# Attention of a two-layer trunk: B projected as 384 columns twice, q and k normalised at another place and by VectorE alone, two chunks of transposed probabilities in one PSUM bank

## The chip, the cores and the metric

One core of one Trainium2 chip runs the whole program in one launch. The metric is the device time of an execution in microseconds (us). The program uses five engines: TensorE (PE in the profile, with its weight loads as PEld), VectorE (DVE), ScalarE (ACT), GpSimd (POOL), and SyncE (SP), which here only issues DMAs.

## The reference, cut to what matters

The input is 512 tokens of width 1024 in float32. Layer 0 has two kinds of attention on one normalised input: A, 8 heads of 64 with a mixture of three dilated windows, and B, 8 query heads over 2 key-value heads, a window of 128 and a learned sink per head. Layer 1 has 16 heads of forgetting attention, called C here. Each layer ends with an MLP of width 4096 with a squared ReLU.

```python
q = rms_norm(q.reshape(bsz, seq, heads, 64), q_gain)   # A, B and C; k in the same way
s = q @ k * 64**-0.5 + bias                            # window, slope, or forget gates
p = exp(s - max(s));  out = (p @ v) / sum(p)           # B: the sink joins max and sum
y = concat(a_out, b_out) @ w_out                       # layer 0; layer 1: c_out @ w_out
x = x + y;  x = x + square(relu(rms_norm(x) @ w_up)) @ w_down
```

So every head of q and k (not v) is divided by its own root mean square before the scores are taken.

## The kernel before, in words

**Number format.** Each float32 operand is split into a high part (`hi`, a cast to fp32r) and a low part (`lo`, the rest), and a product is three matmuls: high by high, low by high, high by low. So weights and activations pass through a cast on ScalarE or GpSimd and a subtraction on VectorE or GpSimd before TensorE can use them (`split` L146, `scale_split` L156).

**Order.** The kernel is traced in Python, and a planner then orders each engine's instructions: every instruction has a priority, by default the order in which it was traced, and the planner takes, engine by engine, the one of the best priority that it thinks is ready, by costs of its own. Instructions marked `keep_in_program_order` stay in traced order; in the attention hardly any are. At run time each engine is strictly in order and waits at the first instruction whose inputs are late. DMAs of weights and of K stand in SyncE's one queue.

**Projections.** `project` (L206) takes some columns of the input weights and gives four banks of PSUM (tag pA, 4 banks in all), one for each 128 tokens. It walks over the 1024 rows in groups of `kw` chunks of 128 (4 chunks for 256 columns, else 2); `load_w` (L177) issues one DMA per group and column range into a raw tile (4 raw tiles in all, `RAW`) and splits it into high and low. The engines of the splits come from a pattern: `PAT_START` casts on ScalarE and subtracts on VectorE, `PAT_ATT` casts on GpSimd and subtracts on VectorE or GpSimd in turn.

**Normalisation.** `norm_heads` (L239) takes the four banks when they are complete. For each it copies the bank to SBUF and squares it, both on ScalarE from PSUM, and sums the squares by head on VectorE (L249). Then come four small scalings (L252), an inverse root by bit trick and three Newton steps on VectorE (`rsqrt_small`, L122, 11 instructions), and four multiplications in place (L259), which `NORM = 'vgvg'` gives to VectorE and GpSimd in turn.

**Attention.** `attend` (L402) goes by pairs of heads. `prep_q` and `prep_k` transpose normalised columns on TensorE into a PSUM bank (tag pB, 4 banks), split them, and for k copy the halves to the other partitions by DMA (L289). `scores` (L301) handles four blocks of 128 queries: scores on TensorE, bias and row minimum of the negated scores on VectorE (L338), exponential with row sum on ScalarE (L341), a reciprocal of that block's sum on VectorE (L344), and a scaling of the probabilities, on GpSimd for blocks 0 to 2 and on ScalarE for block 3 (`PSC = 'ggga'`). `values` (L352) of the head before then transposes the probabilities by chunk of 128 keys: four chunks, four PSUM banks, each with its cast on ScalarE (L373) and subtraction on VectorE (L374); after that it multiplies with V (L381) and evicts (L384, L385). In A and C the chunks 0 to 3 are 512, 384, 256 and 128 columns wide, in B 256, 256, 256 and 128. Chunk 3 is multiplied together with 128 columns of zeros that lie before it in tile `p3`.

**Interleaving.** `run` (L429) traces one attention generator beside one generator of dense matmuls. A dense step counts 32 by its columns over 32 (a projection of n columns counts n in all), an attention step counts one, and `run` keeps `d / n_dense` level with `a / n_att` plus a lead. A step ends at each `yield`: one for each pair, four for the scores of a head, and one for each bank of `values` and its product. In layer 0 the order is: `qk_a(0)` (q and k of A's heads 0 to 3), `v_a(0)`; then attention A of those heads beside `kv_b` (256 columns) and B's q (512 columns); then attention B (`n_att` is `NB` = 86) beside `qk_a(1)` and `v_a(1)` (768 columns); then attention A of heads 4 to 7 beside the output projection. In layer 1 three such runs of C, each beside the projections of the next four heads, and one beside the output projection.

Of the kernel before, what the change touches and what calls it, by code (L numbers as in the profile page):

```python
# [14 lines left out]
OP = mybir.AluOpType  # L15
# [22 lines left out]
NORM = 'vgvg'  # L38
PSC = 'ggga'
GRAIN = 4  # L40
STARTPIN = 4
# [30 lines left out]
def trunk(ctx, tc, x, g_mix, g_mlp, w_in_even, a_q_gain, a_k_gain, b_q_gain, b_k_gain, b_sinks,  # L72
# [45 lines left out]
    ecol = consts.tile([P, NT], F32, name="ecol")  # L118

# [71 lines left out]
    def layer_attention(li, hT, w_in, w_out, stats=None):  # L191


        with ExitStack() as c2:
# [9 lines left out]
            nc.gpsimd.memset(p3[:, :, 256:384].bitcast(F32), 0.0)  # L204
# [34 lines left out]
            def norm_heads(outs, nh, sq_tag="sq", sq_bufs=1 + li):  # L239
# [61 lines left out]
            def scores(q, k, j, kind, h, pr):  # L301
# [11 lines left out]
                rden = small.tile([P, NT], F32, tag="rden", name="rden")  # L313
                for i in range(NT):
# [29 lines left out]
                    nc.vector.reciprocal(rden[:, i:i + 1], den[:, i:i + 1])  # L344
                    if PSC[i] == "a":
                        nc.scalar.activation(p[:, :nv], p[:, :nv], AF.Copy, scale=rden[:, i:i + 1])
                    else:
                        eng = nc.gpsimd if PSC[i] == "g" else nc.vector
                        eng.tensor_scalar(p[:, :nv], p[:, :nv], rden[:, i:i + 1], 1.0, op0=OP.mult, op1=OP.mult)  # L349
                    yield  # L350

            def values(pr, kind, V, vs, yf, j):  # L352

                pts = []
                for c in range(NT):
                    pt = bank("pB", "PT")
                    blocks = [i for i in range(c, NT) if kind != "b" or i <= c + 1]
                    n = len(blocks) * P
                    for i in blocks:
                        kb = c - (max(i - 1, 0) if kind == "b" else 0)  # L360
                        nc.tensor.transpose(pt[:, (i - c) * P:(i - c + 1) * P],  # L361
                                            pr[i][:, kb * P:(kb + 1) * P], ident)
                    if c < 2:
                        d = ap.tile([P, 2, 512 - c * P], F32R, tag=f"PT{c}", bufs=1, name="PT")
                        dst, rhs = d[:, :, :n], d[:, :, :n]
                        cols = slice(c * P, c * P + n)
# [878 lines left out]
```

## Time and profile before

| | |
|---|---|
| median of 3 runs | 1168.81 us (1167.73 to 1170.11) |
| the profiled execution | 1168.43 us |
| its span, first instruction to last | 1166.7 us |
| PE busy / DVE / ACT / POOL | 98% / 75% / 55% / 17% of the span |
| granted TensorE clock | 0.999 in the mean |

The span is the time from the first to the last instruction on the chip; 1.7 us of the execution's time lie around it. Busy shares are averages over stages that differ much. Attention with its projections lies at 28 to 230 us (layer 0) and at 600 to 820 us (layer 1); the MLPs and output projections fill most of the rest. Within layer 0, A's first four heads end at about 105 us, B's heads lie at about 105 to 175 us, and A's last four end at about 210 us. A wait in the view of waits is idle time of an engine before one instruction, with the releaser that came last. Matmuls are pipelined, and their recorded lengths overlap: what one costs TensorE is read from the distance of two starts.

### The profile page before, as it was taken

The numbers are of one execution on the slowest core, as the hardware profiler recorded it, in microseconds if no ns is written. First come the engines' busy times: TensorE is split into PE (matmuls) and PEld (weight loads), VectorE is DVE, ScalarE is ACT, GpSimd is POOL, SyncE is SP. The second block draws the span as 40 slices with busy tenths as digits, with TensorE's granted clock in tenths as the row PEclk, the third lists the DMA queues.
The fourth block names the chain that finished last, engine by engine and source line by source line (L and its number), as shares of the span: only waits on it lengthen the run. The fifth ranks groups of instructions, "written<-read, shape, count | busy, mean of one in ns | idle before, by whom it ended". The sixth has DMA issues, their size and how long they took to land.

```text
span 1166.7 us, 17503 instructions
## 1 busy us (share of the span) xinstructions
PE 1146.8 (98%) x6256; PEld 982.5 (84%) x6256; DVE 880.7 (75%) x1877; ACT 647.1 (55%) x1349; POOL 202.4 (17%) x296
## 2 busy tenths in 40 slices
PE   8999989999999999999999999999999999999998
PEld 7987877888988988988887888888888888888887
DVE  7878999968858857855647877788858759669676
ACT  6555867556545545444235675656756455465452
POOL 1345444200000000000255445332100000000000
PEclk9999999999999999999999999999999999999999
DMA  7522014242333333333443333343430721623403
GB/s 253 163 76 89 19 57 146 70 126 78 104 108 91 91 108 91 106 111 110 146 128 109 107 84 109 107 118 113 163 105 4 235 87 55 198 73 109 147 33 109
DMA packets 100655, 126.57 MB, mean 108 GB/s; under 512 B 6184, under 2 KB 79944, under 8 KB 100568
## 3 DMA queue, kind: packets, MB, share of 16 engines
q1 hardware_dynamic: 99384, 121.23, 34.3%
q10 hardware_dynamic: 608, 2.13, 0.5%
q0 software_dynamic: 576, 2.10, 0.4%
q8 instruction: 49, 0.80, 0.3%
q14 instruction: 38, 0.31, 0.1%
HBM read 112.29 MB, written 6.32 MB: 102 GB/s over the span
## 4 chain that ended last, share of the span: by engine, by line
PE 85%; DVE 8%; DMA 2%; POOL 1%; issue 1%; ACT 1%; SPq 0%; ACTq 0%; POOLq 0%; DVEq 0%
PE up L163 10%; PE up L167 10%; PE up L166 10%; PE pj L230 5%; PE pj L232 5%; PE pj L231 5%; PE O L381 3%; PE PT L361 2%; PE Y L1021 2%; PE Y L1019 2%; PE Y L1022 2%; PE op L167 2%; PE op L163 2%; PE op L166 2%; PE Y L1068 1%; PE S L324 1%
## 5 line engine op out<-in xcount | busy, mean ns | idle before, releaser
L163 PE MATMUL up<-xin,whi 128*128 128x512 f32 x512 | 200.5, 392 | 0.0
L167 PE MATMUL up<-xin,whi 128*128 128x512 f32 x512 | 199.3, 389 | 0.0
L166 PE MATMUL up<-xin,wlo 128*128 128x512 f32 x512 | 199.2, 389 | 0.0
L768 ACT CAST whi<-wraw 128x512 fp32r<-128x512 f32 x228 | 139.2, 619 | 105.0 <-PE up L167 47.7
L769 DVE TENSOR_TENSOR wlo<-wraw,whi 128x512 fp32r<-128x512 f32 x228 | 151.7, 686 | 50.8 <-ACT whi L768 50.5
L167 PEld LDWEIGHTS up<-xin,whi 128*128 128x128 f32 x512 | 96.1, 188 | 20.1
L166 PEld LDWEIGHTS up<-xin,wlo 128*128 128x128 f32 x512 | 96.2, 188 | 19.8 <-issue 0.2
L163 PEld LDWEIGHTS up<-xin,whi 128*128 128x128 f32 x512 | 96.1, 188 | 19.8 <-issue 0.2
L341 ACT ACTIVATE P<-P,negm 128x128 f32<-128x128 f32 (+5 forms) x128 | 69.5, 544 | 51.7 <-DVE negm L338 47.9
L950 ACT ACTIVATE u<-up 128x512 f32<-128x512 f32 x64 | 38.3, 599 | 90.9 <-PE up L167 90.8
L230 PE MATMUL pj<-whi,hn 128*128 128x512 f32 (+2 forms) x256 | 88.7, 346 | 0.0
L232 PE MATMUL pj<-whi,hn 128*128 128x512 f32 (+2 forms) x256 | 86.9, 339 | 0.0
L231 PE MATMUL pj<-wlo,hn 128*128 128x512 f32 (+2 forms) x256 | 86.8, 339 | 0.0
L151 POOL TENSOR_SCALAR whi<-wraw 128x512 fp32r<-128x512 f32 x88 | 60.5, 689 | 143.0 <-PE pj L232 121.8
L789 DVE TENSOR_TENSOR t<-u 128x256 f32<-128x256 f32 x56 | 23.2, 424 | 62.8 <-ACT u L1093 61.0
L154 POOL TENSOR_TENSOR wlo<-wraw,whi 128x512 fp32r<-128x512 f32 x48 | 64.4, 1346 | 20.7 <-ACT whi L149 17.9
L230 PE MATMUL pj<-whi,h 128*128 128x512 f32 (+1 forms) x192 | 66.5, 353 | 0.7 <-DVE v L159 0.7
L232 PE MATMUL pj<-whi,h 128*128 128x512 f32 (+1 forms) x192 | 65.5, 343 | 0.0
L231 PE MATMUL pj<-wlo,h 128*128 128x512 f32 (+1 forms) x192 | 65.5, 341 | 0.0
L349 POOL TENSOR_SCALAR P<-P,rden 128x256 f32<-128x256 f32 (+2 forms) x96 | 47.7, 500 | 90.8 <-DVE rden L344 90.0
L154 DVE TENSOR_TENSOR wlo<-wraw,whi 128x512 fp32r<-128x512 f32 (+1 forms) x72 | 49.9, 700 | 17.7 <-POOL whi L151 14.5
L373 ACT CAST PT<-PT 128x256 fp32r<-128x256 f32 (+3 forms) x128 | 49.5, 405 | 19.4 <-PE PT L361 18.5
(229 smaller groups left out, 3054.4 us busy)
## 6 DMA issues: line engine op xcount, KB each, us to landing
wraw<-in_w_up SPq DMA_DIRECT2D x64, 512.0 KB, 3.8
wraw<-in_w_down SPq DMA_DIRECT2D x56, 512.0 KB, 4.2
wraw<-in_w_in_odd SPq DMA_DIRECT2D x36, 256.0 KB, 3.3
mraw<-in_w_down SPq DMA_DIRECT2D x16, 512.0 KB, 4.4
K<-K SPq DMA_DIRECT2D x26, 256.0 KB
wraw<-in_w_in_even SPq DMA_DIRECT2D x10, 512.0 KB, 4.0
wraw<-in_w_in_even SPq DMA_DIRECT2D x16, 256.0 KB, 4.5
xl<-xsp SPq DMA_DIRECT2D x8, 512.0 KB
```

What stands on the lines that cost most here:

```text
L151: nc.gpsimd.tensor_scalar(dst_h, src, 1.0, 1.0, op0=OP.mult, op1=OP.mult)
L154: in_order((nc.gpsimd if lo == "pool" else nc.vector).tensor_sub(dst_l, src, dst_h.bitcast(F32)))
L163: m = nc.tensor.matmul(o, wh, xh, start=start, stop=False, skip_group_check=more)
L166: nc.tensor.matmul(o, wl, xh, start=False, stop=False, skip_group_check=more)
L167: nc.tensor.matmul(o, wh, xl, start=False, stop=stop, skip_group_check=more)
L230: nc.tensor.matmul(o, xh, hi[:, :n], start=k == 0, stop=False)
L231: nc.tensor.matmul(o, xh, lo[:, :n], start=False, stop=False)
L232: nc.tensor.matmul(o, xl, hi[:, :n], start=False, stop=k == DC - 1)
L341: nc.scalar.activation(p[:, :ne], p[:, :ne], AF.Exp, scale=-1.0, bias=negm[:, i:i + 1], accum_out=den[:, i:i + 1])
L373: nc.scalar.copy(dst[:, 0], pt[:, :n])
L768: sca(nc.scalar.copy(dst_h, src))
L769: late.append(lambda: vec(nc.vector.tensor_sub(dst_l, src, dst_h.bitcast(F32))))
```

## The change

Four edits, all in the attention of both layers.

1. `norm_heads` first copies the four banks (ScalarE). All the rest is traced at once, but under `later(100)`, which raises the priority number by 100: the planner ranks it behind the next 100 traced instructions or so. The squares are taken from the copy in SBUF. The four small scalings become one instruction over all four token blocks, and all four multiplications go to VectorE.
2. B's projection is cut differently. Before: k and v of B (256 columns), then q of B (512 columns). After: q heads 0 to 3 with k (384 columns, `PAT_START`), then q heads 4 to 7 with v (384 columns, `PAT_ATT`). A group of rows then has two DMAs, of 256 and 128 columns.
3. In `scores` the reciprocals and scalings of blocks 0 to 2 come together after block 2's exponential; block 3's follow after its own. A head has two reciprocals where it had four.
4. In `values` A and C put chunks 3 and 2 into one bank, so three banks, casts and subtractions where there were four. B puts chunks 0 and 1 into one and 3 and 2 into another: two where there were four. The zeros in `p3` move to its first 128 columns. A head of A or C has one step fewer, a head of B two fewer; `NB`, `LEADS` and the other counts of `run` stay.

```diff
+    def later(n):
+        tc.cur_priority += n
+        yield
+        tc.cur_priority -= n
...
                 for t in range(NT):
-                    q = qk[t // 2][:, t % 2, :w]
-                    nc.scalar.copy(q, outs[t][:, :w])
-                    sq = ap.tile([P, 512], F32, tag=sq_tag, bufs=sq_bufs, name="sq")
-                    nc.scalar.activation(sq[:, :w], outs[t][:, :w], AF.Square)
-                    nc.vector.reduce_sum(ss[:, t, :nh], sq[:, :w].rearrange("p (h d) -> p h d", d=HD), axis=AX.X)
-                v = small.tile([P, NT, 8], F32, tag="ssv", name="ssv")
-                for t in range(NT):
-                    nc.vector.tensor_scalar(v[:, t, :nh], ss[:, t, :nh], 1.0 / HD, ecol[:, t:t + 1],
-                                            op0=OP.mult, op1=OP.add)
-                rs = small.tile([P, NT, 8], F32, tag="rs", name="rs")
-                rsqrt_small(rs[:, :, :nh], v[:, :, :nh])
-                for t in range(NT):
-                    q = qk[t // 2][:, t % 2, :w].rearrange("p (h d) -> p h d", d=HD)
-                    eng = nc.gpsimd if NORM[t] == "g" else nc.vector
-                    eng.tensor_mul(q, q, rs[:, t, :nh].unsqueeze(2).to_broadcast([P, nh, HD]))
+                    nc.scalar.copy(qk[t // 2][:, t % 2, :w], outs[t][:, :w])
+                with later(LATER):
+                    for t in range(NT):
+                        q = qk[t // 2][:, t % 2, :w]
+                        sq = ap.tile([P, 512], F32, tag="sq", bufs=1 + li, name="sq")
+                        nc.scalar.activation(sq[:, :w], q, AF.Square)
+                        nc.vector.reduce_sum(ss[:, t, :nh], sq[:, :w].rearrange("p (h d) -> p h d", d=HD), axis=AX.X)
+                    v = small.tile([P, NT, 8], F32, tag="ssv", name="ssv")
+                    nc.vector.scalar_tensor_tensor(v[:, :, :nh], ss[:, :, :nh], 1.0 / HD,
+                                                   ecol.unsqueeze(2).to_broadcast([P, NT, nh]), op0=OP.mult, op1=OP.add)
+                    rs = small.tile([P, NT, 8], F32, tag="rs", name="rs")
+                    rsqrt_small(rs[:, :, :nh], v[:, :, :nh])
+                    for t in range(NT):
+                        q = qk[t // 2][:, t % 2, :w].rearrange("p (h d) -> p h d", d=HD)
+                        nc.vector.tensor_mul(q, q, rs[:, t, :nh].unsqueeze(2).to_broadcast([P, nh, HD]))
...
-                    nc.vector.reciprocal(rden[:, i:i + 1], den[:, i:i + 1])
...
+                    ps_.append(p[:, :nv])
+                    if i >= 2:
+                        i0 = 0 if i == 2 else 3
+                        nc.vector.reciprocal(rden[:, i0:i + 1], den[:, i0:i + 1])
+                        for n in range(i0, i + 1):
+                            if PSC[n] == "a":
+                                nc.scalar.activation(ps_[n], ps_[n], AF.Copy, scale=rden[:, n:n + 1])
+                            else:
+                                nc.gpsimd.tensor_scalar(ps_[n], ps_[n], rden[:, n:n + 1], 1.0, op0=OP.mult, op1=OP.mult)
...
+                for cs in (((0, 1), (3, 2)) if kind == "b" else ((0,), (1,), (3, 2))):
+                    pt = bank("pB", "PT")
+                    n = 0
+                    for c in cs:
+                        for i in blocks(c):
+                            kb = c - (max(i - 1, 0) if kind == "b" else 0)
+                            nc.tensor.transpose(pt[:, n:n + P], pr[i][:, kb * P:(kb + 1) * P], ident)
+                            n += P
+                    if cs == (3, 2):
+                        d = p3[:, :, P:]
+                        pts[3] = p3[:, :, :256], slice(256, 512)
+                        pts[2] = p3[:, :, 256:], slice(256, 512)
...
+                    nc.scalar.copy(d[:, 0], pt[:, :n])
+                    nc.vector.tensor_sub(d[:, 1], pt[:, :n], d[:, 0].bitcast(F32))
...
-                def kv_b():
+                def qk_b():
+                    return project([(1536, 1792), (2048, 2176)], qk_use("b0", 6), PAT_START)
+
+                def qv_b():
                     def use(outs):
-                        st["v", 3] = prep_v(outs, P, 2, 1)
-                        st["k", "b"] = norm_heads(outs, 2)
-                    return project([(2048, 2304)], use, PAT_START)
+                        st["v", 3] = prep_v(outs, 256, 2, 1)
+                        st["qk", "b1"] = norm_heads(outs, 4)
+                    return project([(1792, 2048), (2176, 2304)], use)
...
-                run(att_a(0), 32, chain(kv_b(), project([(1536, 2048)], qk_use("b", 8))), 768, LEADS[0])
+                run(att_a(0), 32, chain(qk_b(), qv_b()), 768, LEADS[0])
```

## Rows read from the trace of the kernel before

**Rows 1.** The page's line of busy time, share of the span and instructions of each engine.

```profile
PE 1146.8 (98%) x6256; PEld 982.5 (84%) x6256; DVE 880.7 (75%) x1877; ACT 647.1 (55%) x1349; POOL 202.4 (17%) x296
```

**Rows 2.** The view by stretches: from and to in us, length, then busy us and instruction count of each engine, granted clock, DMA share, GB/s. The first row lies in the last MLP, the others in the attention.

```profile
830.00:1160.00 330.00, 330.00 (x1477) 273.38 (x1476) 241.80 (x391) 177.23 (x322) 0.00 (x0) 1.00 0.33 106
...
44.00:98.00 54.00, 52.46 (x325) 46.12 (x324) 41.75 (x120) 30.76 (x81) 28.77 (x41) 1.00 0.28 79
98.00:110.00 12.00, 10.66 (x56) 8.35 (x55) 9.83 (x22) 3.74 (x7) 6.81 (x8) 1.00 0.43 132
110.00:165.00 55.00, 51.48 (x345) 44.61 (x344) 51.28 (x170) 43.03 (x128) 26.42 (x62) 1.00 0.12 39
165.00:230.00 65.00, 63.74 (x334) 52.67 (x333) 60.41 (x141) 41.55 (x98) 20.63 (x28) 1.00 0.36 106
600.00:640.00 40.00, 38.83 (x199) 31.97 (x198) 26.64 (x71) 20.18 (x44) 21.37 (x26) 1.00 0.36 106
640.00:820.00 180.00, 178.04 (x1108) 152.93 (x1107) 143.34 (x382) 112.41 (x273) 72.72 (x98) 1.00 0.39 110
```

**Rows 3.** The view of waits of TensorE, in 44 to 230 us: who waited for whom, us in total, times, longest.

```profile
PE S L324 <- DVE yf L385: 1.8, 2, 1.6
PE S L324 <- DVE Q L277: 1.8, 2, 1.5
PE qkT L266 <- DVE qk L259: 1.3, 2, 0.9
PE pj L230 <- DVE v L159: 0.7, 1, 0.7
```

**Rows 4.** The same view in 600 to 830 us.

```profile
PE S L324 <- DMA K<-K: 2.6, 3, 1.1
```

**Rows 5.** TensorE's instructions in order of time (start, length): scores of 256, 384 and 512 columns one behind the other.

```profile
56.01 0.28 PE L325 MATMUL S<-K,Q 128*128 128x256 f32 x1
56.12 0.34 PE L324 MATMUL S<-K,Q 128*128 128x384 f32 x1
56.30 0.34 PE L325 MATMUL S<-K,Q 128*128 128x384 f32 x1
56.48 0.39 PE L324 MATMUL S<-K,Q 128*128 128x512 f32 x1
56.71 0.40 PE L325 MATMUL S<-K,Q 128*128 128x512 f32 x1
```

**Rows 6.** The same view a little later: three transposes, then a projection; one transpose, then a projection.

```profile
60.04 0.49 PE L361 MATMUL PT<-ident,P 128*128 128x128 f32 x3
60.29 0.36 PE L230 MATMUL pj<-whi,h 128*128 128x256 f32 x1
60.49 0.28 PE L231 MATMUL pj<-wlo,h 128*128 128x256 f32 x1
...
61.09 0.28 PE L361 MATMUL PT<-ident,P 128*128 128x128 f32 x1
61.13 0.37 PE L230 MATMUL pj<-whi,h 128*128 128x256 f32 x1
61.33 0.28 PE L231 MATMUL pj<-wlo,h 128*128 128x256 f32 x1
```

**Rows 7.** VectorE's groups by shape in 28 to 250 us: count, busy us and mean ns of one, idle before.

```profile
L154 DVE TENSOR_TENSOR wlo<-wraw,whi 128x512 fp32r<-128x512 f32 x26 | 19.1, 737 | 3.5 <-ACT whi L149 2.0 <-POOL whi L151 1.3
...
L344 DVE RECIPROCAL rden<-den 128x1 f32<-128x1 f32 x64 | 10.0, 158 | 2.0 <-ACT P L341 1.3
...
L374 DVE TENSOR_TENSOR PT<-PT 128x512 fp32r<-128x512 f32 x8 | 5.5, 684 | 0.9 <-ACT PT L373 0.9
...
L374 DVE TENSOR_TENSOR PT<-PT,PT 128x128 fp32r<-128x128 f32 x16 | 4.5, 279 | 0.6 <-ACT PT L373 0.6
L374 DVE TENSOR_TENSOR PT<-PT 128x384 fp32r<-128x384 f32 x8 | 4.4, 550 | 0.1
...
L252 DVE TENSOR_SCALAR ssv<-ss,ecol 128x8 f32<-128x8 f32 x12 | 4.1, 351 | 0.1
```

**Rows 8.** VectorE's instructions in order of time: the first multiplication of the norm of `qk_a(0)`; the two of `qk_a(1)` with what follows them.

```profile
44.18 0.69 DVE L259 TENSOR_TENSOR qk<-qk,rs 128x512 f32<-128x512 f32 x1
...
159.11 1.55 DVE L259 TENSOR_TENSOR qk<-qk,rs 128x512 f32<-128x512 f32 x1
...
160.58 1.53 DVE L259 TENSOR_TENSOR qk<-qk,rs 128x512 f32<-128x512 f32 x1
162.21 0.68 DVE L385 TENSOR_TENSOR yf<-O,yf 64x512 f32<-64x512 f32 x1
```

**Rows 9.** GpSimd's and then VectorE's instructions at 614 to 621 us, behind the norm of C's first four heads.

```profile
614.19 2.93 POOL L259 TENSOR_TENSOR qk<-qk,rs 128x512 f32<-128x512 f32 x2 [3.12 <-DVE rs L133]
617.10 0.62 POOL L151 TENSOR_SCALAR whi<-wraw 128x512 fp32r<-128x512 f32 x1
...
619.70 1.09 DVE L154 TENSOR_TENSOR wlo<-wraw,whi 128x512 fp32r<-128x512 f32 x1 [3.47 <-POOL whi L151]
620.81 0.68 DVE L277 TENSOR_TENSOR Q<-qkT,Q 64x512 fp32r<-64x512 f32 x1
```

**Rows 10.** SyncE's own waits over the whole span: what its queue stood at, and for whom.

```profile
SPq L182 <- DVE wlo L154: 110.4, 20, 27.4
SPq L289 <- DVE K L159: 63.9, 24, 16.6
```

More of the change, by code (lines that the diff above doesn't have):

```diff
@@ L1 @@
-from contextlib import ExitStack
+from contextlib import ExitStack, contextmanager
 import numpy as np
@@ L37 @@
 WARM = 24
-NORM = 'vgvg'
 PSC = 'ggga'
 GRAIN = 4
+LATER = 100
 STARTPIN = 4
@@ L118, in trunk @@
     ecol = consts.tile([P, NT], F32, name="ecol")
+    @contextmanager
+    def later(n):
+        tc.cur_priority += n
+        yield
+        tc.cur_priority -= n
     cnt = {"hi": 0, "start": STARTPIN}
@@ L203, in layer_attention @@
             p3 = ap.tile([P, 2, 512], F32R, tag="PT3", name="PT3")
-            nc.gpsimd.memset(p3[:, :, 256:384].bitcast(F32), 0.0)
+            nc.gpsimd.memset(p3[:, :, :P].bitcast(F32), 0.0)
             def project(cols, use, pat=PAT_ATT, ahead=False):
@@ L237, in project, with norm_heads @@
                 yield 0
-            def norm_heads(outs, nh, sq_tag="sq", sq_bufs=1 + li):
+            def norm_heads(outs, nh):
                 w = nh * HD
@@ L313, in scores @@
                 rden = small.tile([P, NT], F32, tag="rden", name="rden")
+                ps_ = []
                 for i in range(NT):
@@ L343, in scores @@
                     pr.append(p)
-                    nc.vector.reciprocal(rden[:, i:i + 1], den[:, i:i + 1])
[L345 to L349, printed above, removed]
+                    ps_.append(p[:, :nv])
@@ L350, in scores, with blocks @@
                     yield
             def values(pr, kind, V, vs, yf, j):
-                pts = []
-                for c in range(NT):
+                def blocks(c):
+                    return [i for i in range(c, NT) if kind != "b" or i <= c + 1]
+                pts = {}
+                for cs in (((0, 1), (3, 2)) if kind == "b" else ((0,), (1,), (3, 2))):
                     pt = bank("pB", "PT")
[L357 to L366, printed above, removed]
-                    elif c == 2:
-                        dst, rhs = p3[:, :, :256], p3[:, :, :256]
-                        cols = slice(256, 512)
-                    else:
-                        dst, rhs = p3[:, :, 384:512], p3[:, :, 256:512]
-                        cols = slice(256, 512)
-                    nc.scalar.copy(dst[:, 0], pt[:, :n])
-                    nc.vector.tensor_sub(dst[:, 1], pt[:, :n], dst[:, 0].bitcast(F32))
-                    pts.append((rhs, cols))
@@ new lines, in values @@
+                    n = 0
[8 more added lines that the diff above has]
+                        pts[2] = p3[:, :, 256:], slice(256, 512)
+                    else:
+                        d = ap.tile([P, 2, 512 - cs[0] * P], F32R, tag=f"PT{cs[0]}", bufs=1, name="PT")
+                        o = 0
+                        for c in cs:
+                            m = len(blocks(c)) * P
+                            pts[c] = d[:, :, o:o + m], slice(c * P, c * P + m)
+                            o += m
@@ L530, in get @@
                         if p_ == 0:
-                            st["kb"] = prep_k(st["k", "b"], 0, gg[:, 1:2])
+                            st["kb"] = prep_k(st["qk", "b0"], 256, gg[:, 1:2])
                         k = st["kb"][p_ // 2]
-                        return prep_q(st["qk", "b"], p_ * P), [k, k]
+                        return prep_q(st["qk", f"b{p_ // 2}"], p_ % 2 * P), [k, k]
                     return attend(get, 0, lambda: st["v", 3], lambda j: j // 4, "b", 0, 4, 4)
```

## The prediction

> **What bounds the kernel now.** I read the page's busy times first: TensorE is busy 98% of the span, the next engine 75% [rows 1]. So the floor is TensorE's own work, and a change of other engines' work can only pay where TensorE waits for them. The view by stretches says where that is [rows 2]. In the last MLP TensorE is busy the whole of 330 us. In the attention it idles 54 - 52.46 = 1.54 us at 44 to 98 us, 1.34 at 98 to 110, 3.52 at 110 to 165, 1.26 at 165 to 230, 1.17 at 600 to 640 and 1.96 at 640 to 820: 10.8 us together. That is all that a change of this kind can win, unless it takes work from TensorE itself. Of the stretches, 110 to 165 us (attention B) is the one that another engine bounds: VectorE is busy 51.28 of 55 us there. TensorE's waits name VectorE for nearly all of it in layer 0, each a few long ones and not many short ones [rows 3], and the DMA that mirrors K in layer 1 [rows 4].
>
> **The change, part by part.**
>
> *TensorE's work: nothing.* The projection of B has 96 matmuls of 256 columns and 96 of 512 before, 192 of 384 after. By the distance of starts, 256 columns take 0.11 us, 384 take 0.18 and 512 take 0.23 [rows 5], so 96 x 0.34 = 32.6 us against 192 x 0.18 = 34.6. These starts are rounded to 0.01 us, and two of 384 have just as many columns as one of 256 and one of 512. I take 0, with 0 to +2 as the bounds. The merged banks change no transpose either, only the grouping. Does a group as such cost TensorE something? Three transposes and the matmul behind them take 0.45 us to the next start, of which a matmul of 256 columns would take 0.12: 0.33, or 0.11 each. One transpose alone costs 0.24 - 0.12 = 0.12 [rows 6]. So the price goes by transposes, and fewer groups give nothing.
>
> *VectorE, per head.* Two reciprocals fewer, 2 x 0.158 = 0.32 us. The subtractions of 128, 384 and 512 columns take 0.279, 0.550 and 0.684 us, so about 0.145 us of each does not depend on its width [rows 7]: one instruction fewer in A and C saves 0.145, two fewer in B 0.29. B's eight heads together: 8 x 0.61 = 4.9 us. A's eight: 8 x 0.47 = 3.7; C's sixteen: 7.4.
>
> *VectorE, per normalisation.* Four scalings at a mean of 0.351 become one of 128x32, which I put at the same 0.35: -1.05 us [rows 7]. Of the multiplications, one that starts alone takes 0.69 us; two that run while GpSimd multiplies take 1.55 and 1.53, so VectorE is held from 159.11 to about 162 us for two [rows 8]. Four without GpSimd's multiplications beside them would be 4 x 0.69 = 2.8 us or a little less. So VectorE multiplies twice as much in the same time, and GpSimd is freed of some 2.9 us [rows 9]. The bounds here are 2.8 us, and 4 x 1.55 = 6.2 if GpSimd's other work meets all four.
>
> The Trainium skill, in "SBUF — State Buffer", section "Who interferes with whom", says that a VectorE instruction with two SBUF inputs contends with a GpSimd instruction that reads SBUF, that the shared pair is an exclusive lock, and that order of issue decides who blocks. The doubled multiplications agree with that. But the rule also speaks against this edit: the weight splits remain on GpSimd and read SBUF, so by it each of the now four multiplications can be blocked by one of these instead. What that would cost is the first of the rivals.
>
> *B's weights.* 12 pieces of 512 columns become 16 of 384. On VectorE the subtractions go from 8 at 0.737 us [rows 7] = 5.9 us to 12 at about 0.6 = 7.2: +1.3 us, at 44 to 98 us, where VectorE is busy 41.75 of 54 us [rows 2]. That spare time covers it; without the cover it costs the 1.3. DMAs go from 6 to 16 for the same bytes, on SyncE's queue. That queue stands mostly at weight loads which wait for a raw tile (110.4 us), and 24 of 26 K copies waited for their own data, not behind a load [rows 10]. So I price the extra DMAs at nothing; the bound is three K copies late by the longest K wait, 3 x 1.1 = 3.3 us [rows 4].
>
> *Where it lies on the path.*
> (a) Start of attention B, 98 to 110 us. TensorE waits 1.3 us for the multiplications of B's q [rows 3], because q's projection ends just before its use. After the change, q of heads 0 to 3 and k come out of the first of the two projections, some 17 us earlier (96 x 0.18), and are normalised long before. What is late next is the split of Q and K, with the rest of the projection to cover it. -1.3 us.
> (b) Attention B, 110 to 165 us. TensorE idles 3.52 us, mostly in a wait for yf of 1.6 and one for Q of 1.5 [rows 3]. The first is the two multiplications at 159 to 162 us, with the eviction L385 right behind them [rows 8]. After the change that norm ranks 100 instructions lower, so an eviction that is ready goes first, and VectorE has 4.9 + 1.05 us less to do in a stretch where it had 3.7 us to spare. TensorE can't win more than its 3.52; I take -2.5.
> (c) 165 to 230 us: four heads of A, VectorE down by 1.9 us, TensorE idle 1.26. I take -0.5.
> (d) 44 to 98 us: the wait of 0.7 us for v [rows 3] stands behind the norm of `qk_a(0)`; against it stands the +1.3 us of weights. I take -0.3.
> (e) Layer 1. The K waits sum to 2.6 us [rows 4]. The first stands behind the norm of C's first heads. GpSimd casts weights only after its two multiplications (at 617.10), VectorE waits 3.47 us for a later cast of GpSimd, and Q's split, for which the scores and K wait, stands behind that at 620.81 [rows 9]. Without GpSimd's multiplications this comes up to 2.9 us earlier, more than the longest wait of 1.1. For the other two I see no such chain. -1.5 us in all, for the smaller waits too.
> (f) The order. The planner arranges every engine anew, and a head has one or two steps fewer with `NB` and `LEADS` as they were, so attention runs ahead of the dense work. Some new wait will come of it. Nothing in the trace prices it; the single waits of rows 3 and 4 are 0.3 to 1.6 us. I take +0.5, bounds 0 and +5.7 (the third rival).
>
> The sum is -1.3 - 2.5 - 0.5 - 0.3 - 1.5 + 0.5 = -5.6 us, from 1168.4 (the profiled execution: 1166.7 of span and 1.7 around it) to 1162.8. That execution is 0.4 under the median of the runs, so as a median 1163.
>
> **The rivals.**
> *GpSimd's other work collides with the multiplications.* If each of them takes 1.55 us, a norm costs VectorE 3.1 to 4 us more than it did, at all eight norms. In attention B that eats most of the 5.9 us it saves, (b) shrinks to -0.5, (e) to -0.5, (c) to -0.2 and (d) to nothing, and the sum is -2.0: 1167 as a median. For it: GpSimd is busy 26.42 of 55 us there [rows 2], and its cast follows its multiplications at once [rows 9]. Against it: only a part of that work falls on any 2.8 us.
> *The waits move and nothing is won.* TensorE is in order; the K copies stay late, and what B's start gives back is lost at another place: 1168 to 1169. For it: the waits are few and long, so each depends on a single place in the order.
> *Attention B runs ahead of its cover.* By the yields, B has 76 steps before (8 x 9 + 4) and 61 after (first head 8, seven of 7, plus 4), against `NB` = 86. So 10/86 of the 768 columns of projection were left over when B ended, and 25/86 are now. By rows 5, 32 pairs of tiles with three matmuls of 512 and three of 256 take 32 x 3 x 0.34 = 32.6 us, so 9.5 us are left over in place of 3.8. If TensorE lacks these 5.7 us beside B, where VectorE sets the pace, and pays them behind B, the sum of the rest (about -5.6 with B's own part of 2.5 not won, so -3.1) turns to +2.6: 1171.4. It decides when VectorE is still over 93% busy in B's stretch and TensorE under 51.48 of 55. For it: VectorE is already the pace there. Against it: the planner pulls ready projections forward whatever the traced order, and VectorE's saving works against it.
>
> **How the numbers follow.** My forecast (1157 to 1166, all of the idle time gone being 1168.4 - 10.8 = 1157.6) gets 0.64, the collision 0.10, no change 0.09, B ahead of its cover with other new waits 0.17. About 0.2%, 2.3 us, is what a measurement of this kernel can tell from no change. The collision at 1167 and no change are within it, so faster 0.65, same 0.17, slower 0.18. The range runs from 1156, a little under the floor of idle time since small waits hide in pipelined matmuls, to 1171.5, just past the slower rival.
>
> **What would show it.** (a) No wait of a transpose for qk at about 105 us. (b) TensorE's idle time in B's stretch about 1 us, VectorE's groups of reciprocals at 64 for both layers, L374's counterpart at 40 in layer 0 and 48 in layer 1 where each had 64. The multiplications at 0.69 us each, or at 1.55 if the collision holds. (e) K waits at or under 1.1 us in sum. The forecast is wrong if TensorE's idle time in the attention stays at 10 us or more, or if its own work grew, that is if it is busy longer in the same matmuls.

## The result, and the profile after

The changed kernel takes 1172.52 us (median of 10 runs, 1171.2 to 1175.39) against 1168.61 us of the kernel before beside it: 1.0037 times the time, with a 95% interval of 1.0029 to 1.0046. It is slower by 3.9 us, where 5.6 us less had been forecast. All medians here are of executions in the fast state; one slow one, of 1259.98 us in `h2_steps_ahead`, is left out. The time lies 1 us above the range, and 1.1 us above the price of the third rival. The profiled execution took 1172.38 us, with a span of 1170.6.

The page's first line after the change answers to [rows 1]:

```profile
PE 1149.0 (98%) x6256; PEld 986.1 (84%) x6256; DVE 873.6 (75%) x1769; ACT 647.9 (55%) x1313; POOL 180.4 (15%) x280
```

VectorE (DVE) has 7.1 us and 108 instructions less, GpSimd (POOL) 22 us less, TensorE the same number of matmuls. So the other engines did become lighter. TensorE's idle time is 1170.6 - 1149.0 = 21.6 us against 1166.7 - 1146.8 = 19.9. The rest of the 3.9 us is in TensorE's busy time, 2.2 us more. Up to 1.7 us of that is a stretch at a lower granted clock, shown in the last section; what the rest is, no row shows. The view by stretches, against [rows 2]:

```profile
44.00:98.00 54.00, 51.66 (x316) 48.69 (x315) 39.77 (x103) 31.60 (x77) 22.88 (x36) 1.00 0.33 93
98.00:110.00 12.00, 11.41 (x58) 9.07 (x57) 10.91 (x28) 4.67 (x11) 6.39 (x8) 1.00 0.45 132
110.00:165.00 55.00, 52.68 (x354) 45.76 (x353) 51.23 (x150) 44.46 (x120) 25.01 (x61) 1.00 0.12 39
165.00:230.00 65.00, 61.32 (x311) 50.56 (x312) 54.83 (x112) 37.02 (x81) 19.14 (x25) 0.97 0.35 106
```

At the start of B (98 to 110 us) the idle time fell from 1.34 to 0.59 us, and in B's stretch from 3.52 to 2.32. Behind B, at 165 to 230 us, it rose from 1.26 to 3.68, and at 44 to 98 us from 1.54 to 2.34. From 44 to 165 us TensorE idles 5.25 us where it idled 6.40, but from 165 to 230 it idles 2.42 us more, with the lower clock on top. So what was won at B was lost behind it. By the first matmul of layer 0's MLP, which starts at 231.9 us after and 229.4 before, 2.5 us of the loss are layer 0's; the other 1.4 come later. TensorE's waits at 44 to 235 us, against [rows 3]:

```profile
PE PT L376 <- DVE negm L346: 2.5, 2, 1.9
PE O L396 <- ACT PT L389: 1.7, 2, 1.5
PE qkT L273 <- DVE qk L266: 1.6, 1, 1.6
PE PT L376 <- POOL P L360: 1.0, 2, 0.7
PE S L332 <- DMA K<-K: 0.6, 1, 0.6
```

The waits for Q and yf of [rows 3] are gone, and these five now lead the view. Two of them in order of time: first the handover from B to A's last four heads. The rows are TensorE's product for B's seventh head, VectorE's multiplications, and TensorE's first transposes for A.

```profile
156.99 0.75 PE L396 MATMUL O<-PT,v 128*128 128x256 f32 x5
...
165.39 2.48 DVE L266 TENSOR_TENSOR qk<-qk,rs 128x512 f32<-128x512 f32 x4
...
166.12 0.44 PE L273 MATMUL qkT<-ident,qk 128*128 128x128 f32 x2 [1.63 <-DVE qk L266]
```

The product of B's seventh head is through at 157.7 us (the eighth head's stands beside A's first heads, at 175.9 to 178.9), and A's heads can't begin before 166, because their q and k, projected beside B, are normalised only then. (The four multiplications take 2.48 us together.) In the kernel before these transposes began no earlier:

```profile
166.29 0.60 PE L266 MATMUL qkT<-ident,qk 128*128 128x128 f32 x4
```

So this wait alone doesn't put the changed kernel behind it; what had been won up to there is gone by it. Second, a product of A's first heads:

```profile
80.43 0.49 PE L376 MATMUL PT<-ident,P 128*128 128x128 f32 x3
80.67 1.06 PE L396 MATMUL O<-PT,v 128*128 128x512 f32 x4
83.26 0.39 PE L396 MATMUL O<-PT,v 128*128 128x256 f32 x1 [1.52 <-ACT PT L389]
```

The three transposes of the merged bank (chunks 3 and 2) are followed at once by the product, whose second half needs that bank's cast. It waits 1.52 us.

### The profile page after: what moved, and what is told of

The parts are those of the page before. It is cut to its first block, busy times and chain, and to the rows that moved or that the text cites. A ratio compares the mean times of both kernels' runs of the same rounds, so it can differ in the third digit from the quotient of the medians.

```text
span 1170.6 us, 17394 instructions
## 1 busy us (share of the span) xinstructions
PE 1149.0 (98%) x6256; PEld 986.1 (84%) x6256; DVE 873.6 (75%) x1769; ACT 647.9 (55%) x1313; POOL 180.4 (15%) x280
## 3 DMA queue, kind: packets, MB, share of 16 engines
q10 hardware_dynamic: 608, 2.13, 0.5%
## 4 chain that ended last, share of the span: by engine, by line
PE 88%; DVE 5%; ACT 3%; POOL 2%; issue 2%; DMA 1%; SPq 0%; POOLq 0%; ACTq 0%
PE up L170 10%; PE up L174 10%; PE up L173 10%; PE pj L237 5%; PE pj L238 5%; PE pj L239 5%; PE O L396 3%; PE op L174 2%; PE op L173 2%; PE op L170 2%; PE PT L376 2%; PE Y L1040 2%; PE Y L1037 2%; PE Y L1039 2%; PE Y L1086 1%
## 5 line engine op out<-in xcount | busy, mean ns | idle before, releaser
L173 PEld LDWEIGHTS up<-xin,wlo 128*128 128x128 f32 x512 | 96.2, 188 | 19.9 <-issue 0.2
L158 POOL TENSOR_SCALAR whi<-wraw 128x512 fp32r<-128x512 f32 (+1 forms) x88 | 56.8, 647 | 201.0 <-PE pj L239 172.8
L161 POOL TENSOR_TENSOR wlo<-wraw,whi 128x512 fp32r<-128x512 f32 (+1 forms) x48 | 65.5, 1367 | 28.1 <-ACT whi L156 19.4
L161 DVE TENSOR_TENSOR wlo<-wraw,whi 128x512 fp32r<-128x512 f32 (+2 forms) x76 | 51.9, 690 | 20.3 <-POOL whi L158 16.1
L237 PE MATMUL pj<-whi,h 128*128 128x512 f32 (+2 forms) x192 | 65.5, 347 | 0.3 <-ACT qk L252 0.3
L239 PE MATMUL pj<-whi,h 128*128 128x512 f32 (+2 forms) x192 | 65.1, 339 | 0.0
L238 PE MATMUL pj<-wlo,h 128*128 128x512 f32 (+2 forms) x192 | 65.0, 339 | 0.0
L346 DVE CUSTOM_DVE_ANT_0 P<-S,bias 128x128 f32<-128x128 f32 (+1 forms) x96 | 45.4, 484 | 20.2 <-PE S L335 17.0
L396 PE MATMUL O<-PT,v 128*128 128x256 f32 (+2 forms) x256 | 57.0, 334 | 3.3 <-ACT PT L389 1.7
```

What stands on the lines that cost most here:

```text
L158: nc.gpsimd.tensor_scalar(dst_h, src, 1.0, 1.0, op0=OP.mult, op1=OP.mult)
L161: in_order((nc.gpsimd if lo == "pool" else nc.vector).tensor_sub(dst_l, src, dst_h.bitcast(F32)))
L173: nc.tensor.matmul(o, wl, xh, start=False, stop=False, skip_group_check=more)
L237: nc.tensor.matmul(o, xh, hi[:, :n], start=k == 0, stop=False)
L238: nc.tensor.matmul(o, xh, lo[:, :n], start=False, stop=False)
L239: nc.tensor.matmul(o, xl, hi[:, :n], start=False, stop=k == DC - 1)
```

## The experiments

Three theories were put up from these rows. **S**: the number of steps fell (a head of A or C has one less, a head of B two less) while the counts of `run` stayed, so attention runs ahead of the dense matmuls that should cover it. **L**: the later place of the norm. **G**: the grouped scalings. A fourth, **D**, is the spacing between a head's last bank and its product; **O** holds that any new order of the planner's is a draw worth several us. Diffs are against the changed kernel unless it says otherwise. Medians are in us; each is set against runs of the kernel before on the same chip. These differ by 0.7 us from chip to chip (1167.9 to 1168.6), so a difference of that size between two runs is not read as an effect. Each trace is of one execution, which can lie up to 3.1 us from the median.

**The former step counts, and LATER = 0** (`e4_step_counts`, `e1_no_later`).

```diff
                     nc.vector.tensor_sub(d[:, 1], pt[:, :n], d[:, 0].bitcast(F32))
-                    yield
+                    for c in cs:
+                        yield
```

```diff
-LATER = 100
+LATER = 0
```

> The changed kernel, but a merged bank ends as many steps as it has chunks, so that attention keeps its former counts (B 76 steps, not 61); the work is the same. Theory S (the lower step counts let attention run ahead of the projections, so that the second A group waits for its projection and norm at 166 us): 1172.5 falls to 1168 or below, the projection of q and k of A's heads 4 to 7 ends near 137 us again instead of 145, and the transposes' wait of 1.6 us for qk goes. Theory L (the norm's later place) and theory G (the grouped scalings): 1171 to 1173, those waits stay.

> The changed kernel with LATER = 0: the norm ranks where it is traced. Theory L (the norm, ranked 100 instructions later, is late for the transposes that follow): about 1170, the norm of A's heads 4 to 7 ends before 164 us instead of 168, and the wait of 1.6 us of qkT for qk goes. Theory S: 1172 or more, since the projection itself ends 8 us late. Theory G: no change, 1172.5.

With the steps back: 1163.88, ratio 0.9959 (0.9947 to 0.9972). Not one instruction of work differs from the changed kernel, and it is 8.6 us faster than that and 4.7 faster than the kernel before. Layer 0's MLP starts at 225.3 us. The view by stretches for the same two stretches:

```profile
110.00:165.00 55.00, 53.44 (x364) 47.07 (x365) 51.66 (x153) 45.81 (x122) 26.23 (x61) 1.00 0.12 39
165.00:230.00 65.00, 64.70 (x331) 53.71 (x330) 57.21 (x118) 40.59 (x88) 19.29 (x25) 1.00 0.35 106
```

TensorE's idle time behind B falls from 3.68 to 0.30 us, and its wait for the normalised q and k is gone. The expectation missed one detail: A's projection ends at 141.1 us, not at 137. Even so the transposes for A start at 161.8 us, where the changed kernel had 166.1. LATER = 0 alone gives 1172.06, and a wait of 1.5 us for q and k stays: L falls as the cause.

**One scaling per block, and four banks** (`e2_per_block`, `e3_four_banks`).

```diff
-                    if i >= 2:
-                        i0 = 0 if i == 2 else 3
-                        nc.vector.reciprocal(rden[:, i0:i + 1], den[:, i0:i + 1])
-                        for n in range(i0, i + 1):
+                    if True:
+                        nc.vector.reciprocal(rden[:, i:i + 1], den[:, i:i + 1])
+                        for n in (i,):
```

```diff
-                for cs in (((0, 1), (3, 2)) if kind == "b" else ((0,), (1,), (3, 2))):
+                for c in range(NT):
...
+                    nc.scalar.copy(dst[:, 0], pt[:, :n])
+                    nc.vector.tensor_sub(dst[:, 1], pt[:, :n], dst[:, 0].bitcast(F32))
+                    pts.append((rhs, cols))
+                    yield
```

> The changed kernel with one reciprocal and one scaling per block, as before the change. Theory G (three scalings in a row on GpSimd come late for the transposes): the waits of PT for GpSimd's P (1.0 us by the waits, 2.2 us with what the pipelining hides, at 58 and 127 us) go, 1170.5; VectorE has 128 reciprocals again, +10 us of its time. Theories S and L: 1172 to 1174.

> The changed kernel with one bank per chunk of transposed probabilities, as before the change, so that the step counts are the former ones too. Theory S: as with the counts alone, 1168 to 1169, a little more for the 24 and 16 more subtractions and casts. A fourth theory M (a merged bank is cast and subtracted later, and the product O waits for it, 1.7 us at 81 us and 1.0 at 639 us): 2 us lower than the run with the former counts and merged banks. Theories L and G: 1172 or more.

1169.72 and 1169.9. The first is 2.8 us better, near what G had said, but its waits for GpSimd's P are 1.5 us, not less, so G's mechanism isn't what moved it, as far as a trace of its slowest execution (1172.79) can tell; what did stays open. The second has the former counts by itself and is 2.6 us better than the changed kernel, but 6.0 us worse than merged banks with those counts. So M, which would have had it 2 us better than that, falls; S, with 1168 to 1169, had the merged banks worth too little.

**Counts or spacing?** (`h1_steps_end`, `h2_steps_ahead`). The first gives the steps back behind the product. The second has them between the banks, and raises the five counts of `run`.

```diff
                 nc.vector.tensor_add(yf[r], po[:HD], yf[r])
                 yield
+                for _ in range(2 if kind == "b" else 1):
+                    yield
```

```diff
-NB = 86
+NB = 107
...
+                    for c in cs:
+                        yield
...
-                run(att_a(0), 32, chain(qk_b(), qv_b()), 768, LEADS[0])
+                run(att_a(0), 35, chain(qk_b(), qv_b()), 768, LEADS[0])
```

> The changed kernel with the missing steps given back behind the product of values instead of between its banks: the counts are the former ones (B 76), but nothing stands between the last bank's transposes and the product. Theory S (it is the counts, the share of projection beside attention): about 1164, as with the steps between. Theory D (it is the spacing: a step of dense matmuls between the last merged bank and the product covers its cast and subtraction): 1168 to 1172, with waits of O for PT of 3 us or more in sum against 0.9.

> The changed kernel with the former steps between the banks, but with the five counts of run raised (86, 32, 36, 38, 42 to 107, 35, 40, 44, 48), so that attention runs ahead as far as in the changed kernel. Theory S: 1170 to 1175, the transposes of the second A group wait for their norm again. Theory D: 1164 to 1166, waits of O for PT at or under 1 us.

1165.76 and 1170.01 (1167.69 to 1174.54). With the counts restored and no spacing, 6.8 of the 8.6 us come back. With the spacing and attention ahead, only 2.5 do. So S is the larger part, by both runs. The other 1.9 us (1165.76 - 1163.88) are not shown to be D: its sign was 3 us or more of waits of O for PT, and they are 1.1 us, against 0.9 with the steps between. Layer 0's MLP starts at 225.7 us, as good as with the steps between, so the difference lies behind that; the waits at 600 to 830 us are other ones for the most part:

```profile
PE S L332 <- DMA K<-K: 1.5, 2, 0.7
PE S L332 <- DVE negm L346: 1.0, 1, 1.0
PE O L396 <- DVE PT L390: 0.8, 1, 0.8
```

In the second run, whose trace is of its fastest execution, the transposes' wait for the norm, which S had expected, is only 0.2 us; but a wait of 1.9 us of the transposes for VectorE's minimum at 192 us, which the changed kernel has and the runs with former shares have not, is there again.

**The kernel before, made to run ahead** (`f3_before_ahead`): the counts 86, 32, 36, 38, 42 become 107, 35, 40, 44, 48. The diff is against the kernel before.

```diff
-NB = 86
+NB = 107
...
-                    run(att_c(g), 36, chain(qk_c(g + 1), v_c(g + 1)), 768, LEADS[3 + g])
+                    run(att_c(g), 40, chain(qk_c(g + 1), v_c(g + 1)), 768, LEADS[3 + g])
```

> The kernel before the change with its five counts raised in the same ratio (86, 32, 36, 38, 42 become 107, 35, 40, 44, 48), so that its attention runs ahead of the projections as it does in the changed kernel; no other edit. Theory S: slower than before by 4 to 8 us, 1173 to 1177, with the projection of A's heads 4 to 7 ending some 5 us later than 137 us. Theory O: no sign, within 3 us of 1168.6.

1175.42, ratio 1.0063 (1.0049 to 1.0077): 7.5 us slower, by five numbers. Its waits at 44 to 235 us answer to [rows 3]:

```profile
PE qkT L266 <- DVE qk L259: 2.9, 3, 1.7
PE S L324 <- DMA K<-K: 2.0, 3, 1.5
```

Transposes wait for normalised q and k 2.9 us where it was 1.3: attention is ready for heads whose projections are not. A detail was missed here too: the projection ends at 139.8 us, 2.9 us late and not 5. But not all of the loss is waiting. Layer 1 has a long wait too, and behind it TensorE's granted clock is low:

```profile
PE PT L361 <- DVE negm L338: 2.6, 1, 2.6
```

```profile
652.00:654.00 2.00, 0.37 (x2) 0.37 (x3) 1.97 (x6) 0.33 (x2) 2.00 (x2) 0.75 0.00 0
654.00:656.00 2.00, 2.00 (x9) 1.48 (x8) 1.90 (x7) 1.05 (x5) 0.98 (x3) 0.50 0.01 4
656.00:658.00 2.00, 2.00 (x12) 2.00 (x11) 0.68 (x4) 1.48 (x5) 0.12 (x1) 0.50 0.15 55
658.00:660.00 2.00, 2.00 (x10) 1.94 (x10) 0.76 (x3) 0.79 (x4) 0.47 (x1) 0.55 0.23 76
```

That is up to 3.4 us there, and up to 1.7 more at 106 to 112 us, of the 8.8 us between the two profiled executions (1177.27 and 1168.43).

**The counts scaled down instead** (`f2_nb_69`, `f1_all_counts`, `k1_counts_grain_2`). The share of projection is as before the change, without a step added: `NB` alone; all five counts; and these with a finer grain.

```diff
-GRAIN = 4
+GRAIN = 2
...
-NB = 86
+NB = 69
...
-                    run(att_c(g), 36, chain(qk_c(g + 1), v_c(g + 1)), 768, LEADS[3 + g])
+                    run(att_c(g), 32, chain(qk_c(g + 1), v_c(g + 1)), 768, LEADS[3 + g])
```

> The changed kernel with NB = 69 in place of 86 (86 x 61/76), nothing else: attention B and its projections end together again. Theory S, which holds that B running ahead of its cover is what costs layer 0 its time: layer 0 ends near 225 us (first matmul of its MLP up) as with the former counts, against 231.9; layer 1 keeps its time, so 1166. A rival, theory O (any other order of the planner's would have moved the time as much; the former counts are one lucky draw): layer 0 ends anywhere from 226 to 233.

> The changed kernel with all five counts of run scaled to the lower step counts (86, 32, 36, 38, 42 become 69, 29, 32, 33, 37). Theory S: within 2 us of the run with the former steps, 1162 to 1166. Theory O: anywhere from 1163 to 1173.

> The run with the five counts scaled down (1170.4), with GRAIN = 2 in place of 4: a projection yields every 2 pairs of tiles instead of every 4, so that dense matmuls stand behind almost every step of attention instead of every second. Theory P (with 8 steps to a head and dense matmuls behind every second step, these fall at the same places of every head, and none falls between the last bank and the product): 1163 to 1167, with waits of O for PT under 2 us against 5.7. Theory O (each order is a draw): no reason for either, 1164 to 1172.

1168.96, 1170.36 and 1171.82: S had the first two wrong and P the third, and O's wide ranges hold for all three. `NB` = 69 brings layer 0's MLP to 229.5 us, 2.4 of the 6.6 us. With all counts scaled, these are its first waits over the whole span, and the place of the longest:

```profile
PE O L396 <- DVE PT L390: 3.6, 4, 1.4
PE PT L376 <- DVE negm L346: 2.7, 3, 1.5
PE O L396 <- ACT PT L389: 2.1, 4, 0.7
```

```profile
83.98 0.49 PE L376 MATMUL PT<-ident,P 128*128 128x128 f32 x3
84.23 1.05 PE L396 MATMUL O<-PT,v 128*128 128x512 f32 x4
85.95 0.39 PE L396 MATMUL O<-PT,v 128*128 128x256 f32 x1 [0.67 <-ACT PT L389]
...
88.65 0.56 PE L396 MATMUL O<-PT,v 128*128 128x256 f32 x1 [1.43 <-DVE PT L390]
```

The wait for the norm is gone, as S says, but products wait 3.6 + 2.1 = 5.7 us for their last bank, where the run with the steps behind the product has 0.8 + 0.3 = 1.1. That is 4.6 us more. Behind the longest of them the granted clock is low for up to 1.7 us more:

```profile
86.00:88.00 2.00, 1.23 (x6) 0.90 (x6) 2.00 (x2) 0.00 (x0) 1.50 (x2) 1.00 0.00 0
88.00:90.00 2.00, 1.35 (x5) 1.35 (x6) 0.93 (x3) 0.33 (x1) 0.00 (x0) 0.68 0.30 62
90.00:92.00 2.00, 2.00 (x8) 2.00 (x8) 0.69 (x1) 0.87 (x2) 0.03 (x1) 0.50 0.57 200
```

The two profiled executions are 6.2 us apart (1172.24 and 1166.06), the medians 4.6. So here the products' waits, D, with the clock behind them take what the share gave; that is read from the two traces. Finer grains of projection (P) did not bring it in: these waits are 6.4 us there.

**A step before the product** (`m1_step_before_product`) tests that account: share and spacing, by one step more right before the product, `NB` = 78 and LATER = 0.

```diff
+                yield
                 po = bank("pB", "O")
```

> The changed kernel with LATER = 0 and one step more per head, right before the product of values, and NB = 78 for B's 69 steps (86 x 69/76); A and C have their former counts by it. Theory S with D (share of projection beside attention, and a step between the last bank and the product): 1162 to 1165, waits of O for PT at or under 1.5 us. Theory O: 1164 to 1171.

1164.18, as S with D expected; its waits of O for PT are 0.5 us. The test is weak: O's range holds it too, and in A and C the steps of this kernel are the same as in the one with the former steps and LATER = 0 below, so only B tells anything new.

**How far the lead matters, and how much is a draw** (`f4_steps_no_later`, `j2_steps_nb_92`, `m2_steps_nb_80`, `g4_steps_later_50`). All four have the former steps, as the first run above. LATER is 0, 0, 0 and 50, and `NB` 86, 92, 80 and 86; the second of them reads:

```diff
-LATER = 100
+LATER = 0
...
-NB = 86
+NB = 92
```

> The changed kernel with the former step counts and LATER = 0. If the later place of the norm is worth something where the cover is right: 1165 to 1167 against 1163.9. If it is worth nothing, as the run of LATER = 0 alone had it: 1163.4 to 1164.4.

> The changed kernel with the former steps and LATER = 0 (1162.7), and NB = 92 in place of 86: B's 76 steps end at 83% of their projections instead of 88%, and at 71% in the changed kernel. Theory S, taken in proportion (6.5 us for the step from 88% to 71% in all runs together): +1 to +2 us, 1164 to 1165. Theory O: anywhere from 1161 to 1168.

> The changed kernel with the former steps and LATER = 0 (1162.7), and NB = 80: B's 76 steps end at 95% of their projections, where 86 gives 88% (1162.7) and 92 gives 83% (1164.1). Theory S, if it goes on in proportion: 1161 to 1162.5. If 88% is already enough cover: 1162.5 to 1165.

> The changed kernel with the former steps and LATER = 50: between 1163.9 (LATER = 100) and 1162.7 (0), with the same work, counts and spacing in all three. Theory S and D: 1162 to 1165. Theory O, which holds that any new order moves the time by several us: outside of that.

LATER = 0, 50 and 100 give 1162.69, 1164.03 and 1163.88; the first is under both ranges of its expectation. The three ran on three chips, and as ratios to the kernel before they are 0.9960, 0.9961 and 0.9959, each give or take 0.0013. So the later place of the norm is worth nothing here, and a cost of it is not shown either. That these three orders agree speaks against O as the cause of 8.6 us. It does not put the draw at nothing: `NB` = 80, 86 and 92 (LATER = 0) give 1166.19, 1162.69 and 1164.08, and 1166.19 is outside both ranges that were given for it. So of these three leads 86 is the best for 76 steps, S's proportion holds on one side only, and a change of order alone can cost some 3 us. LATER = 0 with the former steps, which the next runs start from, takes 0.996 of the time before (0.9947 to 0.9972), as little as with LATER = 100. Its waits of TensorE at 44 to 230 us are these, 3.8 us, where the five rows of the changed kernel above sum to 7.4:

```profile
PE PT L376 <- DVE negm L346: 3.0, 3, 1.5
PE PT L376 <- POOL P L360: 0.5, 2, 0.3
PE op L174 <- DVE y L161: 0.3, 1, 0.3
```

**The other edits, undone one by one from that version** (`g1_pool_norm`, `g2_old_b`, `j1_per_block`; the last by the diff of the scalings above).

```diff
-                        nc.vector.tensor_mul(q, q, rs[:, t, :nh].unsqueeze(2).to_broadcast([P, nh, HD]))
+                        (nc.vector, nc.gpsimd)[t % 2].tensor_mul(q, q, rs[:, t, :nh].unsqueeze(2).to_broadcast([P, nh, HD]))
```

```diff
-                run(att_a(0), 32, chain(qk_b(), qv_b()), 768, LEADS[0])
+                run(att_a(0), 32, chain(kv_b(), project([(1536, 2048)], qk_use("b", 8))), 768, LEADS[0])
```

> The changed kernel with the former steps and LATER = 0 (1162.7), and with the four multiplications of a norm on VectorE and GpSimd in turn, as before the change. By the prediction's terms (b) and (e), in which VectorE alone saves the collision: 1164.5 to 1166. If these multiplications were never on the path: 1162 to 1163.5.

> The changed kernel with the former steps and LATER = 0 (1162.7), and with B projected as before the change (k and v in 256 columns, then q in 512). By the prediction's term (a): 1164 or more, with a wait of 1.3 us or so of the transposes for q at the start of B. If the planner hides that elsewhere: 1162 to 1163.5.

> The changed kernel with the former steps and LATER = 0 (1162.7), and with one reciprocal and one scaling per block as before the change. Theory G (grouped scalings on GpSimd come late, 1.2 us of waits at 58 us and 0.4 to 1.0 at 126 us in all the runs with grouped ones): 1160.5 to 1161.5, these waits gone. If VectorE's 64 more reciprocals (10 us of its time) weigh more: 1163.5 to 1166.

1165.69, 1167.73 and 1164.53: multiplications by VectorE alone are worth 3.0 us, B's new cut 5.0, the grouped scalings 1.8 (2.7, 4.7 and 1.7 against the kernel before on each one's chip). The first two came as the prediction's terms had it, and G is wrong here too. With B's old cut TensorE's longest wait is the one the prediction named:

```profile
PE qkT L273 <- DVE qk L266: 1.6, 1, 1.6
```

These three and the 6.0 us for merged banks (undone from the version with LATER = 100) add up to 15.8 us, far more than the 5.2 that this version is ahead of the kernel before (1167.9 - 1162.69). So they don't add. That each undoing also leaves the other edits in an order that nobody chose for them would explain it, but is not shown.

## Why the prediction was wrong

**The step that failed is term (f)**, the price of the new order: "I take +0.5, bounds 0 and +5.7". The lower step counts and what they do to the order cost 8.6 us (1172.52 - 1163.88). That the steps cost it is shown, since nothing else differs between these two kernels. How is shown in part: 6.8 us come back with the counts alone, behind the product, which is the share of dense work beside attention, the third rival's mechanism; where the other 1.9 come from stays open. Up to 1.7 of the 8.6 us are the low clock behind a wait at 194 us, and a cost of waits beyond their length was in no term of the prediction. The rival was given 0.17 and a price 1.1 us under the result. That its price came so near is in part luck, for its place was wrong: it looked for the idle time within B's stretch, where VectorE stayed as busy as it had said (51.23 of 55 us, 93%), but TensorE idled less there (52.68 busy, not under 51.48). The loss came behind B: a wait of 1.6 us for heads not yet normalised at 166 us, and one of 1.9 us at 194 us with the low clock behind it. That attention had by then run ahead of the output projection fits the counts, but is argued, not shown.

**Terms (a) to (e)** summed to -6.1 us. The changed kernel with its former steps is the run to hold against them: -4.7. In layer 0, up to the MLP, 229.4 - 225.3 = 4.1 us against 4.6 forecast for (a) to (d). From that point to the end of the span, 1166.7 - 229.4 = 937.3 us became 1162.1 - 225.3 = 936.8: 0.5 us against the 1.5 of (e), so that term was too large, as far as one execution of each shows. The waits for K of [rows 4] did go in the changed kernel, as the view of the same stretch shows, but others took their place:

```profile
PE PT L376 <- DVE negm L346: 1.6, 1, 1.6
PE O L396 <- DVE PT L390: 1.2, 2, 0.8
PE S L332 <- DVE negm L346: 0.4, 1, 0.4
```

**(a)** The wait for B's q at 105 us went, as said. **(b)** The multiplications take 0.683 us in the mean and not 1.55, so the first rival, the collision, has fallen: at 28 to 250 us GpSimd's other work does not meet them often enough. By the rule of the Trainium skill ("SBUF — State Buffer", section "Who interferes with whom") any of them could have been blocked by GpSimd, and the longest of the 32, at 616 us beside a GpSimd subtraction of 1.83 us, did take 1.775 us; but it names what may collide, and how often it does is in the order. VectorE's rows after, in 28 to 250 us, against [rows 7]:

```profile
L390 DVE TENSOR_TENSOR PT<-PT 128x512 fp32r<-128x512 f32 x16 | 11.0, 690 | 3.9 <-ACT PT L389 3.7
...
L266 DVE TENSOR_TENSOR qk<-qk,rs 128x512 f32<-128x512 f32 x8 | 5.0, 683 | 0.0
...
L355 DVE RECIPROCAL rden<-den 128x3 f32<-128x3 f32 x16 | 2.7, 170 | 0.9 <-ACT P L349 0.8
```

A reciprocal of three columns costs 0.170 us where one cost 0.158, and the saving by merged instructions is of the size that was worked out, or more: the one small scaling, put at 0.35 us, takes 0.19. TensorE's work didn't change either: 192 projections of 384 columns start 0.17 to 0.18 us apart (82.67, 82.84, 83.02 in the run with the former steps), half of the distances of 256 and 512 columns together.

What stays open: why scaling the counts leaves a product right behind its last bank while steps added elsewhere do not, and what the steps between the banks give beyond the counts. The planner's order was read from traces, not derived. That the four edits' worth doesn't add was seen and not taken apart.

## What to carry to other kernels

In a kernel whose work is interleaved by counted steps, an edit that saves steps moves everything else: give the steps back before judging the edit. Here the same instructions took 1172.5 or 1163.9 us by that alone, while setting the counts anew (1168.96 and 1170.36) did not bring it back. When merged work leaves fewer places to yield, look in the trace for a consumer right behind its last producer, as the product behind its last bank in the run with all counts scaled. And price the order by a trial of the order: the same five numbers, put into the kernel before, cost it 7.5 us.

## What the runs showed of the hardware that was not expected

A wait can cost more than its length. In the changed kernel two instructions of VectorE with two inputs in SBUF run beside GpSimd's two subtractions at 190 us. They take 1.78 and 1.76 us, where the median of the first one's kind is 0.689 and the mean of the second one's, at 28 to 250 us, 0.796. TensorE waits for the row minimum behind them. VectorE's rows, and GpSimd's:

```profile
190.38 1.78 DVE L312 SCALAR_TENSOR_TENSOR bias<-dist,lt 128x512 f32<-128x512 f16 x1
192.08 1.76 DVE L161 TENSOR_TENSOR wlo<-wraw,whi 128x512 fp32r<-128x512 f32 x1
```

```profile
190.32 2.97 POOL L161 TENSOR_TENSOR wlo<-wraw,whi 128x512 fp32r<-128x512 f32 x2
```

The view by stretches of the next microseconds (TensorE's busy us stand behind the length, the granted clock behind POOL's count):

```profile
192.00:194.00 2.00, 0.95 (x8) 0.62 (x6) 1.97 (x3) 0.00 (x0) 1.29 (x1) 1.00 0.36 78
194.00:196.00 2.00, 1.18 (x9) 0.96 (x9) 1.59 (x7) 1.11 (x4) 0.00 (x0) 1.00 0.43 102
196.00:198.00 2.00, 1.90 (x7) 1.21 (x5) 1.92 (x6) 2.00 (x7) 0.52 (x2) 0.53 1.08 377
198.00:200.00 2.00, 2.00 (x9) 1.76 (x9) 1.37 (x6) 1.65 (x4) 0.87 (x2) 0.61 0.87 308
200.00:202.00 2.00, 2.00 (x14) 1.79 (x13) 1.01 (x3) 1.22 (x4) 0.00 (x0) 1.00 0.00 0
```

TensorE was busy 2.13 of 4 us, and then its granted clock was 0.53 and 0.61, that is mostly the lower of its two levels (1.2 GHz), for some 4 us. At 0.53 and 0.61 it did the work of 2.28 of these 4 us, so up to 1.7 us were lost behind a wait of 1.9. The run with the former steps has no such stretch at 165 to 230 us, where its clock is 1.00. Nor is it alone in this: of the twenty traces, nine have such a stretch in the attention, each of up to 1.7 us or, once, 3.4 (the changed kernel, `e1`, `e2`, `e3`, `f1`, `f2`, `f3`, `j1` and `k1`), and eleven have none (the kernel before, `e4`, `f4`, `g1`, `g2`, `g4`, `h1`, `h2`, `j2`, `m1` and `m2`). It goes with the time: all but `j1` of the nine have medians of 1168.96 us or more, all but `h2` of the eleven medians of 1168.61 or less.
